# A hybrid decoder layer on one core: the gate row of the residual applied after the output projection, gate rows by row sums through memory, merges on VectorE, and two blocks of the output projection computed channel by channel

## The chip, the cores and the metric

The kernel runs on one core of a Trainium2 chip. The metric is the device time of one execution in microseconds (us), the median over runs. A profile is one further execution, recorded instruction by instruction; its own time, and the span of its instructions, are given beside the runs below.

The engines, as the profile names them: PE is TensorE (matmuls, transposes), PEld its weight loads, DVE is VectorE, ACT is ScalarE, POOL is GpSimd, and SP is the engine from which most transfers (DMA) are issued.

## The reference, cut to what matters

One decoder layer for 512 tokens of width 1024, all in float32. A conditioning vector `c` gives six rows of 1024 numbers, `mod = c @ w_ada + b_ada`: shift, scale and gate of each of the two sub-layers. Two causal attention branches of eight heads each (a forgetting softmax, FoX, and a stick-breaking one, sb) read one input projection.

```python
mod = c @ w_ada + b_ada
sh1, sc1, gt1, sh2, sc2, gt2 = split(mod, 6)
u = x * (1.0 + sc1) + sh1
q_a, k_a, v_a, f_a, q_b, k_b, v_b, g_a, g_b = split(u @ w_in)
y_fox = forgetting_attention(q_a, k_a, v_a, log_sigmoid(f_a + b_forget))
y_sb = stick_breaking_attention(q_b, k_b, v_b)
merged = sigmoid(g_a) * (y_fox @ w_fox_proj) + sigmoid(g_b) * (y_sb @ w_sb_proj)
attn_out = merged @ w_o
x = layer_norm(ALPHA * x + (1.0 + gt1) * attn_out, ln1_g, ln1_b)
u2 = x * (1.0 + sc2) + sh2
h_gate, h_val = split(causal_depthwise_conv(u2 @ w_up, conv_w, conv_b))
ffn_out = (silu(h_gate) * h_val) @ w_down
x = layer_norm(ALPHA * x + (1.0 + gt2) * ffn_out, ln2_g, ln2_b)
```

The gate row `1 + gt1` multiplies the columns of `attn_out`, so it may as well multiply the columns of `w_o`; the same holds for `1 + gt2` and `w_down`.

## The kernel before, in words

**Precision.** Every operand of a large matmul is split into a rounded high part (ScalarE, `hi_of`, L75) and the remainder (VectorE, `lo_of`, L78), and each product is three matmuls, high by high, high by low and low by high (`mm3`, L110 to L112). A tile of weights (128x1024 raw numbers, from SP through four buffers `raw`) thus costs one pass of ScalarE and one of VectorE before TensorE can use it (`wh`, `wl`, three buffers).

**Stages in time.** (1) Up to 50 us: shift and scale rows of the first sub-layer by row sums on VectorE (`mod_col`, L164: multiply a 128x1024 tile of transposed `w_ada` with the broadcast `c`, sum along the row, L169, add the bias, L172), and the first input projections. (2) Up to 302 us: sixteen heads, stick-breaking first. Each head has three steps: `stage_a` (scores and softmax or stick-breaking weights), `stage_b` (transposes of the weights and their split), `stage_c` (product with v). Between the steps `fill` issues a set number of matmuls from `stream`, a list of generators: the remaining projections (`proj`), the gate projections (`add_gate`, 24 matmuls each, then a sigmoid), and the branch projections (`bproj`, 12 matmuls each). `lim` says how far the list may be used at each head. (3) The rest of the list, then the output projection with its layer norm by blocks of 128 tokens (`o_main`), each block transposed back (`o_turn`), to 410 us. (4) The up-projection, 44 tiles of 24 matmuls, to 652 us. (5) The down-projection and the second layer norm.

**The gate rows.** `ada_proc` handles the 32 remaining tiles of `w_ada`, one item of the weight stream each. Items 8 to 23 are row sums for shift and scale of the second sub-layer. Items 0 to 7 (first gate) and 24 to 31 (second gate) are accumulated on VectorE into a 128x512 tile, two half-tiles per item (L525, L530); `ada_split` splits the sum into two parts, and `ada_sum` adds it up over the 128 partitions with two matmuls against a matrix of ones (L548, L549), adding the bias row (L551). That leaves the gate row in every partition (`gt`).

**Output projection.** GpSimd multiplies each of the eight weight tiles of `w_o` by `gt` (`wo_proc`, L576) before the split. GpSimd also adds the two gated branches (`merge`, L676), whose result is split into `mh` and `ml`, eight channel tiles. `o_main(i)` then runs 48 matmuls for block i, channel after channel (L819 to L821), with VectorE's residual and statistics behind them (L824, L825, L828). The weight tiles of `w_down` are multiplied by the second gate row on GpSimd in the same way (L588).

**What sets the order.** A scheduler lays out each engine's instructions once, at build time; only SP's transfers keep the order of the program. Engines run their own list in order, and wait for each other by semaphores. VectorE and ScalarE serve the heads and the weight stream from one list each, so a weight tile or a row sum that stands ahead of a head's tile in that list is done first.

Of the kernel before, what the change touches and what calls it, by code (L numbers as in the profile page):

```python
# [45 lines left out]
def layer_kernel(ctx: ExitStack, tc: tile.TileContext, out, xT, x, cT, crow, wa0, wa1, bcol, bgt, w1, wct, wv, bf,  # L46
# [36 lines left out]
    cTs = const([P, KT], F32, "cTs")  # L83
    bcols = const([P, 4, KT], F32, "bcols")
# [7 lines left out]
    onesr = const([P, P], F32R, "onesr")  # L92
    V.tensor_copy(onesr, ones)
# [9 lines left out]
    modc = const([P, 4, KT], F32, "modc")  # L103
    modr = const([P, 4, KT, 2], F32, "modr")
# [70 lines left out]
    def first_load(j):  # L175
# [17 lines left out]
        if j == 1:  # L193
            nc.sync.dma_start(cTs, cT)
            nc.sync.dma_start(bfs, bf)
        pend[j] = [wa, xt, r]

    def first_acc(j):
        wa = pend[j][0]
        if j == 0:  # L200
            for q in (1, 3):
                V.tensor_scalar_add(bcols[:, q, :], bcols[:, q, :], 1.0)
        mod_col(0, j, wa[0], 2 if j == 0 else 1)
        return mod_col(1, j, wa[1], 2 if j == 0 else 1)
# [20 lines left out]
    def first_mod(j):  # L225
        wa, xt = pend[j][0:2]
        sh, sc = modc[:, 0, j : j + 1], modc[:, 1, j : j + 1]
# [281 lines left out]
    def gt_tile(i):  # L509
        t = cons.tile([P, D], F32, name=f"gt{i}", tag="gt")  # L510
        nc.sync.dma_start(t, bgt[i : i + 1, :].broadcast_to([P, D]))
        return t

    gt = [None, None]
    ada_st = {}

    def ada_proc(n):
        def f(r):
            if 8 <= n < 24:
                mod_col(2 + (n - 8) // 8, n % 8, r)  # L520
                return
            g, q = n // 4, n % 4
            if q == 0:
                ada_st[g] = z(F32, "ac2")
                V.tensor_scalar_mul(ada_st[g], r[:, 0:512], cTs[:, 0:1])  # L525
            acc = ada_st[g]
            for e in range(2):
                k = 2 * q + e
                if k > 0:
                    V.scalar_tensor_tensor(acc, r[:, e * 512 : (e + 1) * 512], cTs[:, k : k + 1], acc, ALU.mult, ALU.add)  # L530
        return f

    def ada_split(g, n):
        weights(n, 0)
        acc = ada_st[g]
        ah, al = z(F32R, "ach"), z(F32R, "acl")
        hi_of(ah, acc)
        lo_of(al, acc, ah)
        ada_st[g] = ah, al
        yield 0  # L540

    def ada_sum(g):
        ah, al = ada_st.pop(g)
        ps = bank()
        i = 0 if g < 2 else 1
# [496 lines left out]
```

## Time and profile before

| | |
|---|---|
| median of 3 runs | 779.21 us (778.69 to 779.27) |
| the profiled execution's own time | 776.24 us |
| its span of instructions | 774.2 us |
| PE busy | 755.8 us (98%) |
| DVE busy | 554.2 us (72%) |
| ACT busy | 351.1 us (45%) |
| POOL busy | 144.5 us (19%) |

The page has the busy time of each engine, groups of instructions by line with the mean time of one, the waits (who waited for whom), the chain that ended last, and each engine's timeline. A matmul of 512 columns is recorded with some 0.39 us, since matmuls overlap; what it takes of TensorE is the distance to the next one. TensorE's granted clock stands in the tables by stretch of time, where 1.00 is full speed.

### The profile page before, as it was taken

Reading aid. Unit: us, or ns where it says so; the run is one execution under the profiler, and the core shown is the slowest. Engines: PE = TensorE matmul, PEld = TensorE weight load, DVE = VectorE, ACT = ScalarE, POOL = GpSimd, SP = SyncE. Lnnn points to the kernel's source line nnn. Section 1 sums busy time; section 2 is a strip of 40 time slices with the busy share of each in tenths; the row PEclk is TensorE's granted clock in tenths of the full one; section 3 lists DMA queues with packets and bytes.
Section 4 is the critical chain, followed back from the end, with each engine's and each line's share of the span. In section 5 each row is a group of like instructions: output and inputs, shape, how many; then the busy total and the mean of one; then the engine's idle time right before and its main releaser. Section 6 shows DMA issues by size and latency. Waiting matters only on the chain.

```text
span 774.2 us, 9555 instructions
## 1 busy us (share of the span) xinstructions
PE 755.8 (98%) x3567; PEld 625.0 (81%) x3567; DVE 554.2 (72%) x854; ACT 351.1 (45%) x584; POOL 144.5 (19%) x106
## 2 busy tenths in 40 slices
PE   8998999999999999998999999999999999999995
PEld 5886887888888888886889888888888888888885
DVE  6979999966687876666656887777666665534666
ACT  3357596727666564444125334444444433222300
POOL 1030002001010012363000680000000043945500
PEclk9999999999999999999999999999999999999999
DMA  8961254353333324544301615353332314332302
GB/s 316 403 207 33 78 187 134 119 193 105 113 107 109 136 82 136 166 166 155 118 1 55 218 56 162 109 190 136 110 108 82 109 54 164 113 105 83 108 28 81
DMA packets 30960, 99.41 MB, mean 128 GB/s; under 512 B 4257, under 2 KB 4769, under 8 KB 30914
## 3 DMA queue, kind: packets, MB, share of 16 engines
q1 hardware_dynamic: 30402, 98.74, 37.4%
q8 instruction: 28, 0.46, 0.2%
q0 software_dynamic: 512, 0.07, 0.1%
q14 instruction: 18, 0.15, 0.1%
HBM read 96.62 MB, written 2.10 MB: 128 GB/s over the span
## 4 chain that ended last, share of the span: by engine, by line
PE 77%; DVE 8%; ACT 6%; DMA 3%; issue 3%; POOL 2%; DVEq 0%; POOLq 0%; ACTq 0%; SPq 0%
PE ps L110 14%; PE ps L111 14%; PE ps L112 14%; PE ps L253 5%; PE ps L935 5%; PE ps L934 5%; PE ps L933 5%; PE ps L496 2%; DVE wl L78 2%; ACT wh L75 2%; PE ps L820 2%; PE ps L821 1%; PE ps L478 1%; PE ps L819 1%; DMA raw<-in_wo 1%
## 5 line engine op out<-in xcount | busy, mean ns | idle before, releaser
L78 DVE TENSOR_TENSOR wl<-raw,wh 128x1024 fp32r<-128x1024 f32 (+2 forms) x106 | 145.8, 1375 | 99.8 <-ACT wh L75 99.4
L75 ACT ACTIVATE wh<-raw 128x1024 fp32r<-128x1024 f32 (+2 forms) x106 | 110.3, 1041 | 109.3 <-PE ps L935 38.4
L110 PE MATMUL ps<-u2h,wh 128*128 128x512 f32 (+1 forms) x376 | 141.4, 376 | 0.0
L111 PE MATMUL ps<-u2l,wh 128*128 128x512 f32 (+1 forms) x376 | 141.2, 376 | 0.0
L112 PE MATMUL ps<-u2h,wl 128*128 128x512 f32 (+1 forms) x376 | 141.2, 375 | 0.0
L588 POOL TENSOR_TENSOR raw<-raw,gt 128x1024 f32<-128x1024 f32 x22 | 60.3, 2755 | 190.1 <-DVE gt L551 157.6
L110 PE MATMUL ps<-uh,wh 128*128 128x512 f32 x232 | 92.6, 399 | 0.0
L112 PE MATMUL ps<-uh,wl 128*128 128x512 f32 x232 | 90.9, 392 | 0.0
L111 PE MATMUL ps<-ul,wh 128*128 128x512 f32 x232 | 90.7, 391 | 0.0
L111 PEld LDWEIGHTS ps<-u2l,wh 128*128 128x128 f32 x376 | 70.8, 188 | 12.9
L110 PEld LDWEIGHTS ps<-u2h,wh 128*128 128x128 f32 x376 | 70.8, 188 | 12.8
L112 PEld LDWEIGHTS ps<-u2h,wl 128*128 128x128 f32 x376 | 70.8, 188 | 12.8
L112 PEld LDWEIGHTS ps<-uh,wl 128*128 128x128 f32 x232 | 43.6, 188 | 9.3
L110 PEld LDWEIGHTS ps<-uh,wh 128*128 128x128 f32 x232 | 43.6, 188 | 8.3 <-ACT pt L454 0.3
L111 PEld LDWEIGHTS ps<-ul,wh 128*128 128x128 f32 x232 | 43.7, 188 | 8.0
L934 PE MATMUL ps<-wl,hh 128*128 128x512 f32 x128 | 49.8, 389 | 0.0
L933 PE MATMUL ps<-wh,hh 128*128 128x512 f32 x128 | 49.8, 389 | 0.0
L935 PE MATMUL ps<-wh,hl 128*128 128x512 f32 x128 | 49.8, 389 | 0.0
L75 ACT ACTIVATE hh<-cv 128x512 fp32r<-128x512 f32 x22 | 13.9, 632 | 59.6 <-DVE cv L913 59.6
L912 ACT ACTIVATE cv<-cv 128x512 f32<-128x512 f32 x22 | 13.9, 632 | 54.8 <-DVE cv L907 54.8
L576 POOL TENSOR_TENSOR raw<-raw,gt 128x1024 f32<-128x1024 f32 x8 | 20.1, 2517 | 80.9 <-DVE m L78 42.2
L906 DVE SCALAR_TENSOR_TENSOR cv<-ps,cw,cv 128x511 f32<-128x511 f32 x44 | 32.7, 743 | 2.3 <-ACT cv L905 2.3
(190 smaller groups left out, 1449.8 us busy)
## 6 DMA issues: line engine op xcount, KB each, us to landing
raw<-in_wup SPq DMA_DIRECT2D x44, 512.0 KB, 3.3
raw<-in_wa SPq DMA_DIRECT2D x32, 512.0 KB, 3.3
raw<-in_wct SPq DMA_DIRECT2D x29, 512.0 KB, 3.8
raw<-in_wdn SPq DMA_DIRECT2D x22, 512.0 KB, 3.2
wa<-in_wa SPq DMA_DIRECT2D x14, 512.0 KB, 7.3
raw<-in_wp SPq DMA_DIRECT2D x8, 512.0 KB, 3.2
raw<-in_wo SPq DMA_DIRECT2D x8, 512.0 KB, 4.2
raw<-in_w SPq DMA_DIRECT2D x7, 452.0 KB, 8.0
```

The lines of the kernel that those rows point to most:

```text
L75: S.activation(o, i, AF.Copy, scale=scale)
L78: return V.tensor_tensor(o, i, fl(hi), ALU.subtract)
L110: PE.matmul(ps, wh, ah, start=first, stop=False)
L111: PE.matmul(ps, wh, al, start=False, stop=False)
L112: PE.matmul(ps, wl, ah, start=False, stop=last)
L253: PE.matmul(grp[g], w, u, start=j == 0 and n == 0, stop=j == KT - 1 and n == (1 if g == 7 else 2))
L576: G.tensor_tensor(r, r, gt[0], ALU.mult)
L588: G.tensor_tensor(r, r, gt[1], ALU.mult)
L906: V.scalar_tensor_tensor(t[:, 1:], ps[:, 0:511], cw[:, n, 1:2], t[:, 1:], ALU.mult, ALU.add)
L933: PE.matmul(ps, hh[j][:, tb], w[0], start=first, stop=False)
L934: PE.matmul(ps, hh[j][:, tb], w[1], start=False, stop=False)
L935: PE.matmul(ps, hl[j][:, tb], w[0], start=False, stop=last)
```

## The change

The first gate row is no longer multiplied into the weights: `wo_proc` only splits, and `o_main` multiplies the finished product in PSUM by the gate row on VectorE, 128x512 at a time. Both gate rows are now computed like the other rows, by `mod_col`: one row sum of 128x1024 per item. That leaves the row as a column of 128 partitions by 8; `gt_tile` writes it to memory with a transfer on GpSimd's queue and reads it back broadcast to all partitions with a second one. The accumulation, split and ones-matmuls are gone. The second gate row is still multiplied into `w_down` by GpSimd. The sum of the branches moves from GpSimd to VectorE. The five gate projections that stood between the branch projections now stand ahead of them. The output projection of blocks 0 and 1 is done channel by channel in four PSUM banks (`o_part`), 12 matmuls per channel, two places behind the branch projection that makes the channel; blocks 2 and 3 stay in `o_main`. `o_main(2)` moves ahead of `o_turn(0)`.

```diff
-    onesr = const([P, P], F32R, "onesr")
-    V.tensor_copy(onesr, ones)
...
         if j == 0:
-            for q in (1, 3):
-                V.tensor_scalar_add(bcols[:, q, :], bcols[:, q, :], 1.0)
+            V.tensor_scalar_add(bcols[:, 2:6, :], bcols[:, 2:6, :], 1.0)
...
-    def gt_tile(i):
-        t = cons.tile([P, D], F32, name=f"gt{i}", tag="gt")
-        nc.sync.dma_start(t, bgt[i : i + 1, :].broadcast_to([P, D]))
+    MODS = (4, 1, 3, 5)
+    rows = ctx.enter_context(tc.tile_pool(name="rows", bufs=1, space=bass.MemoryType.DRAM))
+
+    def gt_tile(w):
+        row = rows.tile([1, D], F32, name=f"row{w}", tag=f"row{w}")
+        t = cons.tile([P, D], F32, name=f"gt{w}", tag="gt")
+        with nc.allow_non_contiguous_dma("one row of 1024 numbers"):
+            G.dma_start(row.rearrange("o (k p) -> p (o k)", p=P), modc[:, w, :])
+        G.dma_start(t, row.broadcast_to([P, D]))
         return t
...
     def ada_proc(n):
         def f(r):
-            if 8 <= n < 24:
-                mod_col(2 + (n - 8) // 8, n % 8, r)
-                return
-            g, q = n // 4, n % 4
-            if q == 0:
-                ada_st[g] = z(F32, "ac2")
-                V.tensor_scalar_mul(ada_st[g], r[:, 0:512], cTs[:, 0:1])
-            acc = ada_st[g]
-            for e in range(2):
-                k = 2 * q + e
-                if k > 0:
-                    V.scalar_tensor_tensor(acc, r[:, e * 512 : (e + 1) * 512], cTs[:, k : k + 1], acc, ALU.mult, ALU.add)
+            w, col = MODS[n // KT], n % KT
+            mod_col(w, col, r)
+            if col == KT - 1 and w > 3:
+                gt[w - 4] = gt_tile(w)
         return f
-    def ada_split(g, n):
...
-    def ada_sum(g):
...
     def wo_proc(r):
-        G.tensor_tensor(r, r, gt[0], ALU.mult)
...
     def merge(j):
         def f(m):
-            G.tensor_tensor(m, m, ma[j], ALU.add)
+            V.tensor_tensor(m, m, ma[j], ALU.add)
...
+    wos, acc2 = [], []
+
+    def o_step(ps, i, e, k):
+        tb = slice(i * P, (i + 1) * P)
+        PE.matmul(ps, mh[k][:, tb], woh[k][e], start=k == 0, stop=False)
+        PE.matmul(ps, mh[k][:, tb], wol[k][e], start=False, stop=False)
+        PE.matmul(ps, ml[k][:, tb], woh[k][e], start=False, stop=k == KT - 1)
+
+    def o_part(k):
+        if k == 0:
+            acc2.extend([bank(), bank()] for _ in range(2))
+        weights(wos[k], 1)
+        for i in range(2):
+            for e in range(2):
+                o_step(acc2[i][e], i, e, k)
+            yield 6
...
     for j in range(3):
         add_gate(0, j)
     marks["y0"] = len(stream)
-    flush_sum(1 << 30)
+    for j in range(3, KT):
+        add_gate(0, j)
+    skip[0] = 0
+    add_ada(24 - adas[0])
     for j in range(KT):
         add_bproj(0, j, merge(j))
-        if j < 5:
-            add_wo()
-        if j + 3 < KT:
-            add_gate(0, j + 3)
...
+        if j:
+            wos.append(add_item(wo[j - 1], wo_proc))
+            if j > 1:
+                stream.append((o_part, (j - 2,)))
+    wos.append(add_item(wo[KT - 1], wo_proc))
+    for k in (KT - 2, KT - 1):
+        stream.append((o_part, (k,)))
...
-        cut = 6 if i == 0 else KT
-        for e, ks in ((0, range(cut)), (1, range(cut)), (0, range(cut, KT)), (1, range(cut, KT))):
...
+        ps2 = acc2[i] if i < 2 else [bank(), bank()]
         for e in range(2):
             ps = ps2[e]
+            if i > 1:
+                for k in range(KT):
+                    o_step(ps, i, e, k)
+            V.tensor_tensor(ps, ps, gt[0][:, e * 512 : (e + 1) * 512], ALU.mult)
             V.scalar_tensor_tensor(xn[e], xn[e], ALPHA, ps, ALU.mult, ALU.add)
...
-    weights(last_wo, 0)
     o_main(0)
     o_main(1)
+    o_main(2)
     o_turn(0)
-    o_main(2)
     o_turn(1)
...
-            if n in (20, 36):
-                g = 6 if n == 20 else 7
-                list(ada_split(g, wai[4 * g + 3]))
-            if n in (22, 38):
-                list(ada_sum(6 if n == 22 else 7))
```

On the host, the tiles of `w_ada` for the gates are packed transposed like the others, and the bias rows come as one array of six columns.

**How instructions move, first place: VectorE between the first and the third head.** `s_` and `m_` are the split parts of q and k that the next scores wait for, `om_` the stick-breaking factors, `wl_` the low part of a weight tile. Before, q of the second pair of heads, and then its k:

```order
L305 SCALAR_TENSOR_TENSOR fq_542<-ps_110,bfs,fq_541 8x512
L347 SCALAR_TENSOR_TENSOR s_79_559<-ps_105,s_79_559 64x512
L347 SCALAR_TENSOR_TENSOR s_80_562<-ps_105,s_80_562 64x512
L457 SCALAR_TENSOR_TENSOR om_610<-om_610,zer 128x127
L457 SCALAR_TENSOR_TENSOR om_610<-om_610,zer 128x383
```

```order
L78 TENSOR_TENSOR m_2_526<-ps_565,m_114_692 64x512
L78 TENSOR_TENSOR wl_704<-raw_572,wh_703 128x1024
L78 TENSOR_TENSOR m_3_527<-ps_565,m_115_696 64x512
L78 TENSOR_TENSOR vv_713<-ps_106,vv_713 128x2x128
L78 TENSOR_TENSOR vv_716<-ps_107,vv_716 128x2x128
```

The same two pieces of the change:

```order
L342 SCALAR_TENSOR_TENSOR s_79_556<-ps_102,s_79_556 64x512
L166 SCALAR_TENSOR_TENSOR raw_824,modr<-raw_824,cbc 128x1024
L342 SCALAR_TENSOR_TENSOR s_80_559<-ps_102,s_80_559 64x512
L452 SCALAR_TENSOR_TENSOR om_607<-om_607,zer 128x127
L452 SCALAR_TENSOR_TENSOR om_607<-om_607,zer 128x383
```

```order
L78 TENSOR_TENSOR m_2_521<-ps_562,m_114_689 64x512
L78 TENSOR_TENSOR wl_701<-raw_569,wh_700 128x1024
L169 TENSOR_TENSOR modc<-modr,bcols 128x1
L78 TENSOR_TENSOR wl_827<-raw_698,wh_826 128x1024
L78 TENSOR_TENSOR m_3_522<-ps_562,m_115_693 64x512
L78 TENSOR_TENSOR vv_710<-ps_103,vv_710 128x2x128
```

The first row sum of a gate (L166 in the change) now stands between the two parts of q, and its bias together with a second weight tile now stands ahead of the second part of k.

**Second place: TensorE at the end of the branch projections.** `yh`/`yl` are the attention result, `ps_3435` and `ps_3473` the last branch projection's bank. Before:

```order
L112 MATMUL ps_3435<-yh_3022,wl_3348 128x512
L819 MATMUL ps_3489<-woh_3032,mh_3058 128x512
L820 MATMUL ps_3489<-wol_3034,mh_3058 128x512
L821 MATMUL ps_3489<-woh_3032,ml_3059 128x512
L819 MATMUL ps_3489<-woh_3070,mh_3119 128x512
```

Now:

```order
L109 MATMUL ps_3473<-yh_3003,wl_3424 128x512
L650 MATMUL ps_3281<-woh_3427,mh_3400 128x512
L651 MATMUL ps_3281<-wol_3429,mh_3400 128x512
L652 MATMUL ps_3281<-woh_3427,ml_3401 128x512
L650 MATMUL ps_3282<-woh_3428,mh_3400 128x512
```

Before, the whole product of block 0 began behind the last branch projection; now three pieces of 12 matmuls are left there, for channels 5, 6 and 7, and blocks 2 and 3 follow.

**Third place: VectorE on block 3**, the last to be normalised (`xn`) and transposed back. Before, the end of that block and the start of the up-projection:

```order
L792 SCALAR_TENSOR_TENSOR mv_3797<-mv_3797 128x1
L78 TENSOR_TENSOR u2l<-uf_740_3808,u2h 128x4x128
L828 TENSOR_SCALAR xn_3738<-xn_3738,mv_3797 128x512
L828 TENSOR_SCALAR xn_3739<-xn_3739,mv_3797 128x512
L78 TENSOR_TENSOR u2l<-uf_741_3809,u2h 128x4x128
L842 TENSOR_SCALAR uf_756_3900<-ps_3898,gm,bm 128x128 x4
```

Now, first the rows around the second half of the block's residual, then the end of the block:

```order
L796 BN_STATS st_3713<-xn_3711 128x6
L78 TENSOR_TENSOR wl_3814<-raw_3805,wh_3813 128x1024
L78 TENSOR_TENSOR wl_3821<-raw_3807,wh_3820 128x1024
L794 TENSOR_TENSOR ps_3717<-ps_3717,gt_1736 128x512
L813 TENSOR_SCALAR uf_730_3784<-ps_3782,gm,bm 128x128
L795 SCALAR_TENSOR_TENSOR xn_3712<-xn_3712,ps_3717 128x512
```

```order
L765 SCALAR_TENSOR_TENSOR mv_3772<-mv_3772 128x1
L78 TENSOR_TENSOR wl_3851<-raw_3809,wh_3850 128x1024
L799 TENSOR_SCALAR xn_3711<-xn_3711,mv_3772 128x512
L799 TENSOR_SCALAR xn_3712<-xn_3712,mv_3772 128x512
L166 SCALAR_TENSOR_TENSOR raw_3848,modr<-raw_3848,cbc 128x1024
L813 TENSOR_SCALAR uf_748_3881<-ps_3879,gm,bm 128x128 x4
```

The splits of the first three tiles of `w_up` (`wl_3814`, `wl_3821`, `wl_3851`), which VectorE had done ahead of block 0, now stand around block 3; the multiplication by the gate row (L794 in the change) stands ahead of each residual, and a row sum ahead of the copies of block 3's transposes (`uf_748`).

71 lines of the change are left out of this document (12 added, 59 removed).

## The prediction, made before the changed kernel had run

> **What bounds the kernel now.** I read the page's busy times and chain first.
>
> ```profile
> span 774.2 us, 9555 instructions
> PE 755.8 (98%) x3567; PEld 625.0 (81%) x3567; DVE 554.2 (72%) x854; ACT 351.1 (45%) x584; POOL 144.5 (19%) x106
> PE 77%; DVE 8%; ACT 6%; DMA 3%; issue 3%; POOL 2%; DVEq 0%; POOLq 0%; ACTq 0%; SPq 0%
> ```
>
> PE is busy for 98% of the span and holds 77% of the chain. VectorE is second with 72%, POOL has 19%: work taken from POOL is worth nothing by itself, and work given to VectorE costs something only where PE then waits. So I went on to PE's waits (total, number, longest).
>
> ```profile
> PE ps L478 <- DVE m L78: 3.3, 1, 3.3
> ...
> PE ps L819 <- ACT woh L75: 1.5, 1, 1.5
> PE ps L819 <- ACT mh L75: 1.2, 1, 1.2
> PE ps L821 <- DVE ml L78: 0.6, 1, 0.6
> PE ps L422 <- DVE m L78: 0.4, 1, 0.4
> ...
> PE ps L820 <- DVE wol L78: 0.3, 1, 0.3
> ```
>
> Two places stand out: 3.3 us before the transposes of the second head pair (L478), and four waits of 3.6 us together at the start of the output projection (L819 to L821), for a merged channel and for a weight tile. Then the stretches of 2 us around both (length; busy us of PE, PEld, DVE, ACT, POOL; granted clock; DMA), and one long stretch.
>
> ```profile
> 72.00:74.00 2.00, 2.00 (x10) 1.91 (x9) 1.91 (x5) 2.00 (x4) 0.00 (x0) 0.50 0.55 203
> 354.00:356.00 2.00, 1.02 (x5) 0.52 (x3) 0.33 (x1) 1.42 (x2) 0.72 (x1) 1.00 0.86 231
> 356.00:358.00 2.00, 1.17 (x4) 0.70 (x5) 2.00 (x3) 1.20 (x3) 0.00 (x0) 1.00 0.95 297
> 358.00:360.00 2.00, 2.00 (x8) 1.54 (x7) 1.30 (x3) 0.00 (x0) 1.22 (x1) 0.62 1.01 367
> 360.00:362.00 2.00, 2.00 (x7) 1.59 (x6) 0.87 (x2) 1.53 (x2) 0.44 (x1) 0.53 0.41 156
> 76.00:126.00 50.00, 50.00 (x261) 42.02 (x259) 46.36 (x73) 38.61 (x69) 3.98 (x8) 1.00 0.36 117
> ```
>
> After each place the clock is granted at half for a while. At 358 to 362 us the missing clock is 2 x 0.38 + 2 x 0.47 = 1.70 us of full speed, so 3.4 us at half; behind the early wait it stands at 0.50. A second price of a wait is thus 1.7 us of PE, and here a stretch with PE busy for only 1.02 and 1.17 of 2 us, with no long wait in it, was followed by it. [...]
>
> **The change part by part.** The sum is made against the profiled execution: 776.24 us, of which 774.2 is span, so 2.0 lies around it; the median of the runs, 779.21, is 3.0 above that execution.
>
> *1. The matmuls against ones go.*
>
> ```profile
> L548 PE MATMUL ps<-ach,onesr 128*128 128x512 f32 x4 | 1.6, 392 | 0.0
> L549 PE MATMUL ps<-acl,onesr 128*128 128x512 f32 x4 | 1.6, 392 | 0.0
> 354.41 0.39 PE L820 MATMUL ps<-wol,mh 128*128 128x512 f32 x1
> 354.64 0.39 PE L821 MATMUL ps<-woh,ml 128*128 128x512 f32 x1
> 357.56 0.50 PE L821 MATMUL ps<-woh,ml 128*128 128x512 f32 x1 [0.61 <-DVE ml L78]
> 364.04 0.39 PE L821 MATMUL ps<-woh,ml 128*128 128x512 f32 x1
> 366.74 0.50 PE L820 MATMUL ps<-wol,mh 128*128 128x512 f32 x1 [0.30 <-DVE wol L78]
> ```
>
> Two matmuls of this size stand 0.23 us apart. Eight go: -1.8 us. The output projection's 192 matmuls are only moved.
>
> *2. End of the branch projections.* Before, from 354.64 to 357.56 three matmuls passed in 2.92 us instead of 0.68, from 364.04 to 366.74 two in 2.70 instead of 0.45: 4.5 us lost, and 1.5 to 1.7 more at half clock; I take -6.0 for both. Whether the change wins that depends on its new covers. A channel's product now comes two places behind its branch projection, so between the end of that projection and the first matmul of its `o_part` lie one more projection and one more `o_part`, 24 matmuls or 5.4 us. VectorE and ScalarE must meanwhile multiply by the gate, add, round and subtract, four passes over 128x512 of about 0.69 (L824's duration, quoted under 5), and one low part of a weight tile:
>
> ```profile
> L78 DVE TENSOR_TENSOR wl<-raw,wh 128x1024 fp32r<-128x1024 f32 (+2 forms) x106 | 145.8, 1375 | 99.8 <-ACT wh L75 99.4
> L576 POOL TENSOR_TENSOR raw<-raw,gt 128x1024 f32<-128x1024 f32 x8 | 20.1, 2517 | 80.9 <-DVE m L78 42.2
> ```
>
> 4 x 0.69 + 1.38 = 4.1 of 5.4 us. POOL's 2.52 us ahead of each `wo` split, the sum of the two, goes as well, which shortens exactly the chain that L819 waited for. If one step still missed, it would be by well under a microsecond; bounds -6.2 and -4.0.
>
> *3. The early wait.*
>
> ```profile
> 71.55 0.70 PE L478 MATMUL ps<-ident,pt 128*128 128x128 f32 x3 [3.27 <-DVE m L78]
> 57.67 0.69 DVE L347 SCALAR_TENSOR_TENSOR s<-ps,s 64x512 fp32r<-64x512 f32 x1 [0.66 <-ACT s L75]
> 68.77 0.67 DVE L78 TENSOR_TENSOR m<-ps,m 64x512 fp32r<-64x512 f32 x1
> 69.36 1.21 DVE L78 TENSOR_TENSOR wl<-raw,wh 128x1024 fp32r<-128x1024 f32 x1
> 70.70 0.69 DVE L78 TENSOR_TENSOR m<-ps,m 64x512 fp32r<-64x512 f32 x1
> L169 DVE SCALAR_TENSOR_TENSOR raw<-raw,cbc 128x1024 f32<-128x1024 f32 x16 | 19.6, 1222 | 7.9 <-DMA raw<-in_wa 7.8
> ```
>
> From 57.67 on VectorE runs without a gap to the second `m` (70.70), for which PE waited. The order puts a row sum (1.22, and 0.08 to read it out) between the parts of q: 0.66 of it fills an idle, the rest, 0.6, delays. A bias of 0.1 and a second weight tile (1.2) come ahead of the second `m`: 1.3. If the first figure partly vanishes at the scans, `m` is 1.6 us late and the wait grows from 3.3 to 4.9. Queued behind it are the scores and their whole head. Against it: the half-speed stretch, set off at the same time as before, would run partly during the longer idle and cost some 0.7 less. I take +1.0; the bounds are +0.3 (the tile is not ready, and the order's row costs little) and +3.3 (1.6 plus another 1.7 of half clock).
>
> *4. The third head.* One more row sum stands ahead of its `m`, 1.3 us at worst, where PE waited 0.4 before; the gate row's own wait at the bank (L551) goes. +0.2 (0 to +1.3).
>
> *5. Block 3.* Three blocks of the layer norm now reach VectorE almost at once.
>
> ```profile
> 402.89 0.40 PE L821 MATMUL ps<-woh,ml 128*128 128x512 f32 x1
> 403.13 1.03 PE L838 MATMUL ps<-ident,xn 128*128 128x128 f32 x8
> 409.76 1.03 PE L838 MATMUL ps<-ident,xn 128*128 128x128 f32 x8
> 407.04 1.00 DVE L828 TENSOR_SCALAR xn<-xn,mv 128x512 f32<-128x512 f32 x2
> L824 DVE SCALAR_TENSOR_TENSOR xn<-xn,ps 128x512 f32<-128x512 f32 x8 | 5.5, 689 | 16.0 <-PE ps L821 16.0
> L825 DVE BATCH_NORM_STATS2 st<-xn 128x6 f32<-128x512 f32 x8 | 5.6, 694 | 0.3
> L842 DVE TENSOR_SCALAR uf<-ps,gm,bm 128x128 f32<-128x128 f32 x16 | 6.0, 391 | 2.2 <-PE ps L838 2.2
> ```
>
> Of block 3, the last matmul ended at 403.29, normalising at 408.04 (4.8 us), and PE came to its transposes at 409.76 without waiting: it had 6.6 us of cover from 403.13. Now the chain has a gate multiplication more (0.69, like L824's row), a weight tile ahead of normalising (1.2, row of 69.36), and VectorE's backlog. A block costs 6 x 0.69 + 1.0 + some 0.3 of small rows = 5.5; a turn 4 x 0.39 + 2 x 0.69, some 2.8, part of which fits into pauses, so 2.5. From the point where block 0's banks are full, 6 matmuls ahead of the end of `o_part(7)`, to the end of block 3's products PE takes 102 x 0.227 + 2 turns of about 1.0 = 25.2 us. VectorE has in that time three blocks (16.5), half of the fourth (2.1), two turns (5.0) and two weight tiles (2.4): 26.0. It ends 0.8 to 1.0 late. So 4.8 + 0.7 + 1.2 + 1.0 = 7.7 against 6.6: a wait of 1.1. I take +1.0; bounds 0 (small rows hide, ScalarE takes more) and +2.8 (1.1 plus 1.7 of half clock, as after the stretches of 354 to 358). Late behind it are only the turn's copies and the first tiles of the second half.
>
> *6. Start of the second half.* A row sum stands ahead of block 3's copies (1.3), which PE's transposes and the remaining columns wait for: PE has the next tiles' matmuls of the other blocks to do. +0.3 (0 to +0.8).
>
> *7. The gate row through memory.* No such write stands in the trace. The nearest rows are of GpSimd's 4 KB rows:
>
> ```profile
> 143.78 0.52 POOL L328 DMA_DIRECT2D m<-chi  x1 [0.29 <-POOL m L326]
> s<-chi POOLq DMA_DIRECT2D x8, 4.0 KB, 2.0
> q0 software_dynamic: 512, 0.07, 0.1%
> ```
>
> 512 packets over 16 transfers are 32 packets each: 0.52 us to issue, 2 us to land. 1024 elements of 4 bytes in as many packets would be 32 times that at most: 17 us on GpSimd, 64 to landing, and the broadcast read behind it; at the least it is like the row itself. The first row's sums are done at about 145 us and the first use is past 370, the second's are done at about 557 and used by the down-projection from about 620 (GpSimd) and 652 on (PE). Decay rows queue behind it on GpSimd, with 50 us to spare. 0; it turns into a cost from some 65 us on. GpSimd's merges and `wo` products, 1.6 and 2.5 us a piece, had lain off the path but for step 2.
>
> Sum: -1.8 - 6.0 + 1.0 + 0.2 + 1.0 + 0.3 = -5.3. Span 768.9, profiled execution 770.9, **median 773.9**, said as 774.
>
> **The rivals.**
>
> *A: no new wait.* ScalarE and the pauses absorb the backlog, and the early `m` is late only by what the half clock gives back: -1.8 - 6.0, span 766.4, **771.4**. For it: PE 50.00 of 50 us busy from 76 to 126 with VectorE at 46.36, so the added rows found no one to delay there. Against: from 57.67 to 70.70 VectorE had no gap.
>
> *B: each new wait brings its half clock.* Steps 3 and 5 at their upper ends: +3.3 + 2.8 instead of +2.0, and 0.2 + 0.3 as before, **778.0**. For it: the row of 354 to 358, where PE was half busy. Against: the 1.5 us wait at 364 to 366 was followed by none.
>
> *C: slower; row sums ahead of the heads.* Six row sums of 1.3 us stand early on VectorE, at the heads of 57 to 131 us, ahead of the tiles that the next scores wait for. If PE waits for each in full, that is 7.8 us and one more half clock 1.7: with -7.8 and block 3's and the second half's 1.3, +3.0, **782.2**. It decides from the point where PE's new waits before 131 us exceed 6.5 us. For it: VectorE at 46.36 of 50 us, 93%. Against: PE waited nowhere in those 50 us, and ran off a lead.
>
> *D: the gate row is late*, or GpSimd is held by it beyond 85 us, so that block 0 or the down-projection stops: each us beyond costs one, and from 6 us on the sum is above no change, **780** and more. For it: elements of 4 bytes. Against: over 60 us of spare at both.
>
> **How the numbers follow.** Forecast 0.55, A 0.15, B 0.15, C 0.10, D 0.05. The forecast's own range is 772 to 776. The range is 771 to 778: A and B stand at its edges, C and D are left out. A measurement of this kernel can tell some 0.2%, 1.6 us, from no change, that is, 777.6 to 780.8. Faster hold the forecast and A with little loss and some of B: 0.74; no change the rest of B and pieces of D: 0.13; slower C and D: 0.13.
>
> **What would show it right or wrong.** Step 1: PE's instructions fall by eight matmuls. Step 2: no wait on `mh`, `ml`, `woh` or `wol`, and granted clock 1.00 at the end of the branch projections. Step 3: the wait at the transposes of the second pair is 4 to 5 us, released by `m` or by a weight tile. Step 5: a wait of about 1 us at block 3's transposes, released by VectorE; VectorE without a gap before it. Step 7: the write's time to landing under 65 us, and no wait on `gt`. The prediction is wrong if PE's waits before 131 us come to more than 8 us in all, if the half rate shows at a third place, or if PE waits for the gate row.

## The result, and the profile after

The changed kernel takes **770.39 us** (median of 4 runs, 769.29 to 770.88), the kernel before on the same chip 778.95 (777.8 to 779.27): a ratio of 0.9891, 95% interval 0.9874 to 0.9908. That is 8.6 us less. Forecast were 774.0 and a gain of 5.2; the time lies 0.6 us under the low end of the range.

The page after: span and instructions, busy times, and the chain that ended last by engine.

```profile
span 768.5 us, 9512 instructions
PE 752.1 (98%) x3559; PEld 624.6 (81%) x3559; DVE 546.5 (71%) x876; ACT 350.4 (46%) x580; POOL 113.0 (15%) x94
PE 91%; DVE 4%; ACT 4%; issue 1%; DMA 0%; DVEq 0%
```

The span fell from 774.2 to 768.5, by 5.7 us. The sum in the prediction gave 768.9 for it. So the sum of the steps came out to 0.4 us, in part by luck, since single terms were off by up to 2.1 us both ways (below), and the miss in the time lies between the profiled executions and the medians: before, the profiled execution (776.24) was 2.7 us faster than the median on the day of the result; after, 770.30 stands against 770.39. PE's share of the chain rose from 77 to 91%.

PE's waits after (total, number, longest):

```profile
PE ps L473 <- DVE m L78: 4.9, 1, 4.9
PE ps L156 <- DMA cbr<-in_crow: 2.5, 1, 2.5
PE ps L416 <- ACT m L75: 0.4, 2, 0.2
PE ps L809 <- DVE xn L799: 0.2, 1, 0.2
```

The four waits of the output projection are gone, all 3.6 us. The early wait grew from 3.3 to 4.9 us, as told. Block 3's transposes waited 0.2 us. In stretches of 2 us (length; busy PE, PEld, DVE, ACT, POOL; granted clock; DMA):

```profile
72.00:74.00 2.00, 0.39 (x2) 0.42 (x3) 1.94 (x4) 1.36 (x5) 0.00 (x0) 0.64 0.62 209
74.00:76.00 2.00, 2.00 (x10) 1.91 (x9) 2.00 (x6) 0.87 (x2) 0.00 (x0) 0.50 0.74 258
76.00:78.00 2.00, 2.00 (x11) 1.48 (x10) 0.58 (x2) 0.76 (x2) 0.00 (x0) 0.50 0.14 57
78.00:80.00 2.00, 2.00 (x11) 1.92 (x10) 2.00 (x5) 2.00 (x6) 0.00 (x0) 0.65 0.00 0
354.00:356.00 2.00, 2.00 (x11) 1.65 (x10) 0.53 (x1) 0.00 (x0) 0.00 (x0) 1.00 0.00 0
358.00:360.00 2.00, 2.00 (x10) 1.68 (x9) 2.00 (x4) 1.64 (x4) 0.00 (x0) 1.00 0.00 0
```

At the end of the branch projections PE is full and its clock whole. Behind the early wait the missing clock is 2 x (0.36 + 0.50 + 0.50 + 0.35) = 3.4 us, so 6.8 us at half rate, two stretches in a row, where before there was one.

Where the 5.7 us came from, by the times at which PE reached the same matmul (from the two traces' rows, before and after):

| stretch | before | after | difference |
|---|---|---|---|
| start to the first transposes after the early wait | 71.55 | 73.61 | +2.1 |
| to the end of the half rate behind it | 76.07 | 79.13 | +1.0 |
| to the last head's last matmul | 302.12 | 303.44 | -1.7 |
| to the output projection's last matmul | 402.89 | 397.61 | -6.6 |
| to the up-projection's last matmul | 645.98 | 640.14 | -0.6 |
| to the last matmul | 766.07 | 760.16 | -0.1 |

That is -5.9 us; 0.2 of it is lost again behind the last matmul. Of the -1.7, 0.9 are the first gate's four ones-matmuls and some 0.4 the third head's wait, which is gone.

### The profile page after: what moved, and what is told of

Read it like the earlier page. It is cut to its first block, busy times and chain, and to the rows that moved or that the text cites. A ratio compares the mean times of both kernels' runs of the same rounds, so it can differ in the third digit from the quotient of the medians.

```text
span 768.5 us, 9512 instructions
## 1 busy us (share of the span) xinstructions
PE 752.1 (98%) x3559; PEld 624.6 (81%) x3559; DVE 546.5 (71%) x876; ACT 350.4 (46%) x580; POOL 113.0 (15%) x94
## 4 chain that ended last, share of the span: by engine, by line
PE 91%; DVE 4%; ACT 4%; issue 1%; DMA 0%; DVEq 0%
PE ps L107 17%; PE ps L108 17%; PE ps L109 17%; PE ps L248 6%; PE ps L898 5%; PE ps L899 5%; PE ps L897 5%; PE ps L491 2%; PE ps L473 2%; PE ps L652 2%; PE ps L650 2%; PE ps L651 2%; PE ps L416 2%; PE ps L417 1%; PE ps L391 1%; ACT wh L75 1%
## 5 line engine op out<-in xcount | busy, mean ns | idle before, releaser
L78 DVE TENSOR_TENSOR wl<-raw,wh 128x1024 fp32r<-128x1024 f32 (+2 forms) x106 | 142.2, 1343 | 120.5 <-ACT wh L75 120.1
L109 PEld LDWEIGHTS ps<-u2h,wl 128*128 128x128 f32 x376 | 70.8, 188 | 12.7
L107 PEld LDWEIGHTS ps<-u2h,wh 128*128 128x128 f32 x376 | 70.8, 188 | 12.7
L558 POOL TENSOR_TENSOR raw<-raw,gt 128x1024 f32<-128x1024 f32 x22 | 60.1, 2747 | 81.0 <-DVE hl L78 50.9
L166 DVE SCALAR_TENSOR_TENSOR raw<-raw,cbc 128x1024 f32<-128x1024 f32 x32 | 39.0, 1219 | 12.0 <-DMA raw<-in_wa 11.9
```

Of the source, the lines that this page charges most:

```text
L78: return V.tensor_tensor(o, i, fl(hi), ALU.subtract)
L107: PE.matmul(ps, wh, ah, start=first, stop=False)
L109: PE.matmul(ps, wl, ah, start=False, stop=last)
L166: V.scalar_tensor_tensor(wt[:, c], wt[:, c], 1.0, cbc[:, c], ALU.mult, ALU.mult, accum_out=raw[:, e : e + 1])
L558: G.tensor_tensor(r, r, gt[1], ALU.mult)
```

## The experiments

Each run was compared with the kernel before on the same chip. "Clock" is the mean over all executions of a kernel of its granted clock.

| kernel | median us | lowest to highest | ratio to before (95%) | clock |
|---|---|---|---|---|
| before, all executions of the three comparisons | 778.42 | 775.72 to 781.26 (61) | | 0.9921 |
| `again`: before, unchanged | 778.35 | 776.80 to 779.66 (12) | 0.9999 (0.9990 to 1.0008) | 0.9928 |
| `after2`: the change, unchanged | 770.03 | 769.32 to 770.91 (4) | 0.9889 (0.9872 to 0.9906) | 0.9932 |
| `o_late2`: order of blocks and gates undone | 769.48 | 769.17 to 770.57 (4) | 0.9887 (0.9872 to 0.9901) | 0.9930 |
| `pool`: both tasks back on GpSimd | 777.20 | 775.97 to 777.96 (12) | 0.9978 (0.9968 to 0.9988) | 0.9920 |
| `late_row`: `o_late2`, merges on GpSimd | 769.37 | 768.80 to 770.75 (5) | 0.9886 (0.9869 to 0.9904) | 0.9928 |
| `late_merge`: `o_late2`, gate times weights on GpSimd | 771.96 | 770.06 to 772.21 (5) | 0.9907 (0.9891 to 0.9923) | 0.9936 |
| `late_both`: `o_late2`, both on GpSimd | 777.51 | 776.04 to 779.27 (12) | 0.9994 (0.9981 to 1.0007) | 0.9895 |
| `late_ones`: before, both tasks on VectorE | 770.54 | 769.69 to 771.64 (6) | 0.9897 (0.9880 to 0.9914) | 0.9940 |
| `skip6`: the change, row sums later | 771.82 | 770.05 to 772.17 (5) | 0.9909 (0.9894 to 0.9923) | 0.9928 |
| `skip6_row`: `skip6`, gate row transposed first | 768.12 | 767.34 to 768.89 (4) | 0.9864 (0.9847 to 0.9881) | 0.9940 |
| `best1`: `o_late2` with both of these | 768.37 | 767.40 to 768.57 (5) | 0.9868 (0.9851 to 0.9885) | 0.9942 |
| `best2`: `best1`, merges on GpSimd | 771.20 | 770.56 to 772.06 (6) | 0.9908 (0.9892 to 0.9924) | 0.9942 |

### What the usual execution of the kernel before has more

The kernel before, unchanged.

> The kernel before, unchanged, to learn what its usual executions have that the profiled one (776.24 us, two stretches of half clock of 3.4 us) had not. Theory G (grid): stretches of half rate lie on a fixed grid of 3.413 us, which begins anywhere against the program; the waits at 68 us and at 354 to 367 us set off two stretches in a lucky position and three or four in others, at 1.7 us each. Then executions near 779 us have a mean granted clock of 0.991 to 0.992 against 0.994 in the profiled one, and spans of 777. Rival E (edges): the 2.7 us are lost at the first loads or outside the span; then the clock is 0.994 in all executions, whatever their time.

Its spans with their clock: executions at a mean clock of 0.994 have a median of 777.7 us (20 of the 61), those at 0.990 and less 778.95 (16). So G holds, in part: slower executions have the lower clock. Over the 61, the clock takes 6.1 us of full speed (the mean of one less the clock, times the span), against 4.8 in the profiled execution and 4.9 in the changed kernel's. At most these 1.3 us of the 2.2 that separate 776.24 from 778.42 are thus accounted for. At most, because this figure also counts the half rate behind the last matmul, where TensorE has no matmul left: 1.4 of the 4.8 us here, and 1.4 to 2.7 us in the fourteen profiled executions. The rest stays open: even the executions at 0.994 are 1.4 us above that profiled one, which was among the lowest of all.

What makes the number of stretches vary is seen where the stretches begin. In the traces' clock records a stretch lasts 3.413 us, and the two in a row in the change 6.827. They begin on a grid of that length: in the profiled execution before, the second stretch begins 286.72 us after the first, 84 times 3.4133, and the half rate behind the last matmul 699.73 us after it, 205 times; in the change the latter begins 692.91 us after the first stretch, 203 times; in `skip6` two stretches begin 109.22 us apart, 32 times. Where the grid lies against the program differs from execution to execution (half rate from 70.92 to 73.17 us in the table). Behind the early wait, from the clock records and PE's first matmul after the wait, in six of the fourteen profiled executions of this study:

| profiled execution | wait, us | PE resumes | half rate begins | stretches |
|---|---|---|---|---|
| before | 3.3 | 71.55 | 71.74 | 1 |
| `skip6` | 3.3 | 71.95 | 73.17 | 1 |
| `best2` | 3.3 | 71.92 | 72.99 | 1 |
| `late_ones` | 3.3 | 71.61 | 71.46 | 2 |
| `skip6_row` | 3.3 | 71.34 | 70.92 | 2 |
| the change | 4.9 | 73.61 | 72.57 | 2 |

In all fourteen, a second stretch followed where PE was still waiting when the half rate set in, and none where it was running again. So a wait of 3.3 us costs one stretch or two, by where the grid falls, and in all seven executions with 4.9 us it cost two. This is what fourteen executions have in common; no run moved the grid on purpose.

### Which part won: the order, or GpSimd's two tasks

First the channel-wise product was undone, and the gate projections put back between the branch projections:

```diff
-    for j in range(3, KT):
-        add_gate(0, j)
     ...
-            if j > 1:
-                stream.append((o_part, (j - 2,)))
+        if j + 3 < KT:
+            add_gate(0, j + 3)
     ...
-        ps2 = acc2[i] if i < 2 else [bank(), bank()]
+        ps2 = [bank(), bank()]
```

> Of the change, only the channel-wise product of blocks 0 and 1 and the place of the five gate projections are undone (both as before: all four blocks after the last branch projection, gates between the projections); gate row on the result, row sums and merges on VectorE stay. Theory O (the cover of 24 matmuls per channel is what won): the waits for a merged channel come back, 3 to 6 us, 774 to 777 us. Rival P (what won is that GpSimd's 2.5 us no longer stand ahead of each weight split, and its 1.6 us not ahead of each merged channel): within 1.5 us of the change, 769 to 772 us, no wait over 0.5 us at the output projection.

769.48 us: theory O, the step as the prediction told it, falls. The only wait over 0.3 us left besides the first load is the early one:

```profile
PE ps L473 <- DVE m L78: 4.9, 1, 4.9
PE ps L156 <- DMA cbr<-in_crow: 2.3, 1, 2.3
PE ps L416 <- ACT m L75: 0.3, 2, 0.2
```

Then the opposite: the new order stays, GpSimd's two tasks come back.

```diff
-            V.tensor_tensor(m, m, ma[j], ALU.add)
+            G.tensor_tensor(m, m, ma[j], ALU.add)
     def wo_proc(r):
+        G.tensor_tensor(r, r, gt[0], ALU.mult)
     ...
-            V.tensor_tensor(ps, ps, gt[0][:, e * 512 : (e + 1) * 512], ALU.mult)
```

> The change with two parts undone: GpSimd adds the branches again and multiplies the first gate row into the weights of the output projection again; the channel-wise product, the row sums and the place of the gates stay. Theory O: the cover of 5.4 us holds GpSimd's merge too, no wait at the output projection over 0.5 us, and block 3 has one pass less: 769.5 to 771.5 us. Rival P: waits for a merged channel or a weight tile of 2 us or more in all come back: 772.5 us or more.

777.20 us. The waits, in this kernel's line numbers (L651 to L653 are the three matmuls of the output projection):

```profile
PE ps L653 <- DVE ml L78: 2.9, 2, 1.5
...
PE ps L652 <- DVE wol L78: 1.2, 2, 0.8
PE ps L651 <- ACT mh L75: 0.7, 1, 0.7
PE ps L651 <- ACT woh L75: 0.6, 1, 0.6
```

5.4 us: a cover of 24 matmuls per channel does not hold GpSimd's work. So the tasks were the cost, on this order as on the old one. Which of the two? On the order of `o_late2`, merges alone on GpSimd:

> The kernel of the run o_late2 (all four blocks after the last branch projection, gates between them, 769.5 us) with the merges back on GpSimd: so of GpSimd's two tasks only the multiplication of the weights by the gate row is taken away. Theory W (the 2.5 us of GpSimd ahead of each weight split are the cost, the merge of 1.3 to 1.6 us is covered): no wait for a weight tile, at most 1.2 us for a merged channel, 769.5 to 771.5 us. Theory M (the merge is the cost): waits for mh and ml of 2 us and more and a stretch of half clock, 773 us or more.

769.37 us and no such wait. And the weights alone on GpSimd:

> The kernel of the run o_late2 with the multiplication of the output projection's weights by the gate row back on GpSimd, merges on VectorE, no multiplication of the result. Theory W: waits for woh and wol of 1.5 to 5 us, 772 to 776 us. Theory M: no such waits, 769 to 770.5 us.

771.96 us, between the ranges of the two theories, but not by waits of 1.5 us and more at the output projection: its trace loses 1.5 us against `late_row` within the first 79 us (0.9 of it before 12 us) and only 0.3 after, at the last weight tile. What moved the start there stays open. So on this order either task alone is hidden, the weights just so. Both together:

> The kernel of the run o_late2 with both tasks back on GpSimd (merges, and the first gate row times the output projection's weights): of the change only the gate rows by row sums through memory are left. With one of the two tasks back, no wait was seen at the output projection (769.4 and 772.0 us). Theory J (the tasks cost only together: GpSimd's 2.4 and 1.3 us stand in each other's way and stretch VectorE's passes): waits at L650 to L652's matmuls of 2 to 5 us come back and the executions spread over 4 us again, 774 to 779 us. Rival R (what took the waits away is that the gate row's accumulation no longer competes with the branch projections' VectorE work): no such wait, 768.5 to 772 us.

777.51 us, and the interval of its ratio holds 1: the row sums, all that is left of the change here, are worth nothing that can be told. Its waits (L651 to L653 again the output projection):

```profile
PE ps L651 <- ACT woh L75: 3.1, 1, 3.1
...
PE ps L651 <- ACT mh L75: 0.8, 1, 0.8
PE ps L653 <- DVE ml L78: 0.6, 1, 0.6
...
PE ps L652 <- DVE wol L78: 0.3, 1, 0.3
```

And the two tasks taken away with nothing else changed in the kernel before:

```diff
     def wo_proc(r):
-        G.tensor_tensor(r, r, gt[0], ALU.mult)
     ...
-            G.tensor_tensor(m, m, ma[j], ALU.add)
+            V.tensor_tensor(m, m, ma[j], ALU.add)
     ...
+            V.tensor_tensor(ps, ps, gt[0][:, e * 512 : (e + 1) * 512], ALU.mult)
```

> The kernel before with two edits only: the gate row multiplies the result on VectorE, and VectorE adds the branches. Gate rows by accumulation and ones-matmuls, order and early head pairs are as before. Theory J: the four waits at the output projection go, 6 us, and with them the spread: profiled execution and median within 1 us of each other, 769 to 772 us, early wait 3.3 us. Rival R: the waits stay, 776 to 779 us. Between the two kernels' medians the row sums' own worth is then seen: 769.5 (o_late2) less this.

770.54 us, ratio 0.9897: two edits give what the whole change gives, and with them the spread shrinks from 5.5 to 2 us and the mean clock rises to 0.9940. That the spread comes from the waits at the output projection would fit, but is not shown: six executions stand here against 61, and `pool`, with 5.4 us of such waits, spreads over only 2.0 us in 12. (The profiled execution was here the slowest of six, 771.64, so the expected 1 us between it and the median was missed by 0.1.)

**Why only together.** ScalarE's rows show it. In all four kernels its list ends in this stage with the same pieces: a tile of the up-projection (`wh<-raw`), the merged channels 5, 6 and 7 (`mh`) with another `wh` between, and behind the last `mh` the last weight tile of the output projection (`woh`). With neither task on GpSimd (`o_late2`):

```profile
346.70 1.06 ACT L75 ACTIVATE wh<-raw 128x1024 fp32r<-128x1024 f32 x1 [1.44 <-DMA raw<-in_wup]
348.10 0.64 ACT L75 ACTIVATE mh<-sg 128x512 fp32r<-128x512 f32 x1 [0.33 <-DVE sg L638]
...
354.04 0.64 ACT L75 ACTIVATE mh<-sg 128x512 fp32r<-128x512 f32 x1 [0.83 <-DVE sg L638]
354.58 1.14 ACT L75 ACTIVATE woh<-raw 128x512 fp32r<-128x512 f32 x2
```

With both (`late_both`):

```profile
354.56 1.06 ACT L75 ACTIVATE wh<-raw 128x1024 fp32r<-128x1024 f32 x1 [3.79 <-DMA raw<-in_wup]
355.53 0.61 ACT L75 ACTIVATE mh<-sg 128x512 fp32r<-128x512 f32 x1
...
364.70 0.63 ACT L75 ACTIVATE mh<-sg 128x512 fp32r<-128x512 f32 x1 [2.66 <-POOL sg L639]
365.24 1.14 ACT L75 ACTIVATE woh<-raw 128x512 fp32r<-128x512 f32 x2
365.91 0.49 PE L651 MATMUL ps<-woh,mh 128*128 128x512 f32 x1 [3.09 <-ACT woh L75]
```

The first row is the key. ScalarE waits for a tile of `w_up`, which nobody needs for another 50 us, because its load came late; the channels that PE needs now stand behind it. Then each `mh` waits for its merge. The last `woh` starts at 354.58 with neither task, at 358.28 with the merges on GpSimd (the `wh` row at 347.00), at 360.81 with the weights there (353.12, so the load is what the weights delay), at 365.24 with both: 3.7, 6.2 and 10.7 us late. Of the 6.2, 1.5 are the late start of that whole trace, so the two alone add up to 8.4, and both together cost more than the sum. The first half of that tile is rounded some 0.6 us after its start. PE reads it at 360.72 with neither task (5.5 us of reserve), at 360.76 and 362.19 with one (1.9 and 0.8 us left), and with both only at 365.91, after 3.1 us of waiting. One task alone stays inside the reserve, both overrun it. This is read from the rows: no run took the `wh` out of ScalarE's way.

The loads of the up-projection's first three tiles were issued from 344.7 us on, in `o_late2` from 339.3. SyncE, which issues them, waits for a free buffer: one with a tile of `w_o` is free when its low part `wol` is made, and that stands behind GpSimd's multiplication. SyncE's waits for `wol` (total, number, longest), first in `o_late2`, then with the weights on GpSimd (`late_merge`; `late_both` has 20.4 us, `late_row` 12.7; totals of the whole run, which do not say how much each load was late by it):

```profile
SPq L123 <- DVE wol L78: 11.3, 4, 4.0
```

```profile
SPq L123 <- DVE wol L78: 21.8, 5, 8.6
```

GpSimd's multiplications also slow VectorE beside them, a pass of 0.69 us to 2.77. Rows by group, `ml` (two operands in SBUF) and the gate multiplication (one in PSUM), in `late_both` from 302 to 372 us, and then `ml` in `o_late2`:

```profile
L78 DVE TENSOR_TENSOR ml<-sg,mh 128x512 fp32r<-128x512 f32 x8 | 11.8, 1478 | 13.6 <-ACT mh L75 13.6
...
L541 DVE TENSOR_TENSOR sg<-ps,sg 128x512 f32<-128x512 f32 x8 | 5.5, 684 | 0.0
```

```profile
L78 DVE TENSOR_TENSOR ml<-sg,mh 128x512 fp32r<-128x512 f32 x8 | 5.5, 689 | 2.2 <-ACT mh L75 2.2
```

The mean of 1478 ns hides two sizes. Of the four rows from 344 us on, three took 0.68 to 0.69 us, as without GpSimd. The fourth took 2.77; it began while a multiplication of weights ran on GpSimd and ended 0.55 us after it:

```profile
346.96 2.40 POOL L547 TENSOR_TENSOR raw<-raw,gt 128x1024 f32<-128x1024 f32 x1 [0.52 <-DMA raw<-in_wo]
347.14 2.77 DVE L78 TENSOR_TENSOR ml<-sg,mh 128x512 fp32r<-128x512 f32 x1 [2.07 <-ACT mh L75]
```

The pass that reads PSUM stayed at 684 ns on average. The kernel before has both kinds of pass beside such multiplications (L576). `ml`, begun at 347.80, took 2.23 us and ended 0.55 us after the multiplication; the pass with an operand in PSUM, begun at 343.52 within the second of two, took 0.68:

```profile
340.62 5.24 POOL L576 TENSOR_TENSOR raw<-raw,gt 128x1024 f32<-128x1024 f32 x2 [3.31 <-DMA raw<-in_wo]
...
347.07 2.41 POOL L576 TENSOR_TENSOR raw<-raw,gt 128x1024 f32<-128x1024 f32 x1
...
343.52 0.68 DVE L570 TENSOR_TENSOR sg<-ps,sg 128x512 f32<-128x512 f32 x1
347.80 2.23 DVE L78 TENSOR_TENSOR ml<-sg,mh 128x512 fp32r<-128x512 f32 x1 [3.60 <-ACT mh L75]
```

With the merges alone on GpSimd `ml` took 688 ns (`late_row`). It comes behind its own merge there, so this does not show what a pass that falls on a merge would take.

### The early wait, and what came of shortening it

The first row sum two places later in the stream, so that it and the second weight tile no longer stand ahead of the second part of k:

```diff
-    skip = [4]
+    skip = [6]
```

> The change, with the first row sum two places later in the stream of weights, so that neither it nor a second weight tile stands ahead of the second part of k of the second pair on VectorE. Theory S (step 3 as told): the early wait falls from 4.9 to about 3.3 us and one of the two stretches of half clock behind it goes in most executions: 1.6 to 3.3 us less than the change, 767 to 769 us. Rival L: the sums, moved later, delay later heads as much: 770 us, with new waits after 82 us.

771.82 us, above the ranges of both theories and no faster than the change (the intervals overlap). In the profiled execution both parts of theory S came true, a wait of 3.3 us and a single stretch, and PE was some 2.5 us ahead of the change from 80 us on. But all of it was lost at once at 181 us, and 1.5 us more behind it:

```profile
PE ps L416 <- ACT m L75: 3.4, 2, 3.2
PE ps L473 <- DVE m L78: 3.3, 1, 3.3
```

with a stretch of half clock behind. That looks like rival L, but the rows before it point elsewhere. VectorE's row sum at 169.66 waited 8.77 us for a tile, and the transfers nearly stood still (last two columns: DMA share and GB/s):

```profile
169.66 1.23 DVE L166 SCALAR_TENSOR_TENSOR raw<-raw,cbc 128x1024 f32<-128x1024 f32 x1 [8.77 <-DMA raw<-in_wa]
...
156.00:158.00 2.00, 2.00 (x11) 1.65 (x10) 1.76 (x3) 0.00 (x0) 0.95 (x1) 1.00 0.57 178
...
160.00:162.00 2.00, 2.00 (x10) 1.66 (x9) 0.44 (x2) 0.66 (x2) 0.00 (x0) 1.00 0.48 27
162.00:164.00 2.00, 2.00 (x10) 1.67 (x9) 0.00 (x0) 0.00 (x0) 0.00 (x0) 1.00 1.10 37
164.00:166.00 2.00, 2.00 (x10) 1.65 (x10) 0.00 (x0) 0.00 (x0) 0.00 (x0) 1.00 0.30 20
...
row<-modc POOLq DMA_DIRECT2D x2, 4.0 KB, 10.8
```

20 to 37 GB/s instead of 178 from 160 to 168 us, the time in which the gate row went to memory number by number (issued at 156.2; 10.8 us to landing is the median of its two writes), while a 512 KB tile asked for at 157.5 was under way. The change's own write, 8 us earlier, shows the same: 25 to 35 GB/s from 152 to 160 us, and 303 and 410 in the two stretches after it. VectorE waited 5.6 us for a tile there, but PE's matmuls went on. To tell this from rival L, the row was transposed first by one small matmul and then written in 8 rows of 512 bytes; the matmul stands at about 302 us.

```diff
+        ps = bank()
+        PE.transpose(ps[0:KT, 0:P], modc[:, w, :], ident)
+        r = const([KT, P], F32, f"rowt{w}")
+        S.activation(r, ps[0:KT, 0:P], AF.Copy)
     ...
-            G.dma_start(row.rearrange("o (k p) -> p (o k)", p=P), modc[:, w, :])
+        G.dma_start(row.rearrange("o (k p) -> (o k) p", p=P), r)
     ...
+    stream.append((row_tr, (4,)))
```

> The kernel of the run skip6 (first row sum two places later, 771.8 us) in which the gate row is first transposed by one small matmul (8x128 from 128x8), so that the transfer to memory writes 8 rows of 512 bytes instead of 1024 single numbers. In skip6 the packets of the other transfers fell from some 70 to 100 per us to 4 to 11 for the 9 us that the row's write took (158.5 to 168), a weight tile landed 9 us late, and PE waited 3.2 us at 181 us with a stretch of half clock behind. Theory Q (the write of single numbers holds up all transfers): the loads run on while the row is written, the wait at 181 us and its stretch go, 766.5 to 768.5 us. Rival V (VectorE's row sums ahead of the first FoX keys are the cause): the wait of about 3 us at 181 us stays, 770.5 to 772 us.

768.12 us, 1.9 less than the change on the same chip (770.03), and their executions do not overlap. Theory Q's time and rows came out, and rival V falls: the same row sums stand ahead of the same keys. The wait at 181 us is gone, and the write lands in 3.9 us instead of 10.8:

```profile
row<-rowt POOLq DMA_DIRECT2D x2, 4.0 KB, 3.9
...
PE ps L473 <- DVE m L78: 3.3, 1, 3.3
```

(The write was also moved, from 156 to 303 us. The run does not separate the two, so that the shape of the write and not its place is what helped is not shown; at its new place the traffic went on at 135 GB/s and more.) This profiled execution had two stretches of half clock behind the same 3.3 us wait where `skip6` had one, as in the table of the grid.

The yardstick of that comparison:

> The changed kernel again, unchanged, as the yardstick on this chip, and for the spread of its executions: by theory G one place with waits is left, so the executions lie within 2 us of each other at a mean clock of 0.992 to 0.994, where those of the kernel before lay 4 us apart at 0.988 to 0.994. 769.5 to 770.9 us.

Its four executions lie within 1.6 us, at a mean clock of 0.992 to 0.994, as G has it.

### Putting the parts together

> The kernel of the run o_late2, with the first row sum two places later and the gate row transposed before it is written. Both worked on the other order (768.1 us). If the parts add: the 769.5 of o_late2 less 1.9: 767 to 768.5 us, early wait 3.3 us, no wait at 180 us.

768.37 us, as expected, and no better than `skip6_row` (768.12): the block order makes no difference here either. These two beat the kernel before by some 10 us, and the change by 2; of these 2, only `skip6_row` was measured beside the change on one chip.

> The kernel of the run best1 with the merges on GpSimd. Theory J says that one task on GpSimd is covered: as best1 within 0.7 us. If VectorE's merge passes were the cheaper way even alone: 0.7 us or more slower than best1.

771.20 us, 2.8 more than `best1`, where at most 0.7 was expected: the expectation failed. The merges alone on GpSimd, covered in `late_row`, are not covered here:

```profile
PE ps L653 <- DVE wol L78: 1.1, 2, 0.9
PE ps L652 <- ACT woh L75: 0.9, 1, 0.9
```

(L652 and L653 are the first two matmuls of the output projection.) Its row sums stand later, and ScalarE's list has the last two weight tiles together behind the last `mh`, at 358.87. So a shift of the list uses up the reserve that hides one task, 1.9 us in `late_row`.

## Why the prediction was right or wrong, step by step

1. **Ones-matmuls, -1.8.** Right: 8 matmuls fewer on PE's count (3567 to 3559). But `late_ones`, which keeps them, is at 0.9897 against 0.9887 for `o_late2`, within the intervals: with the longer early wait that the row sums brought, the gate rows' new way is worth nothing that can be told.
2. **End of the branch projections, -6.0.** The size was right in the profiled executions (-6.6), the reason was not. The step put the gain on the new covers, 24 matmuls per channel, and named GpSimd's 2.5 us only as a help. `o_late2` keeps the gain without the covers, `pool` loses most of it with them. What counted was that both GpSimd tasks left a chain that, on the order of `o_late2`, had room for one.
3. **The early wait, +1.0.** The wait came out at 4.9 us to the tenth, released by `m` as told. The term was mis-sized by the clock: the half rate was expected to overlap the longer idle and cost 0.7 less; it came twice. That is +3.1 in all by PE's times, near the upper bound of +3.3; 0.3 of it was lost in the first 13 us already.
4. **The third head, +0.2.** No wait remains there: some 0.4 us were won instead.
5. **Block 3, +1.0.** Measured 0.2. The order of events was right, the backlog was not there: VectorE was idle before block 2's second half and began the end of block 3 0.2 us after its products.

```profile
385.39 0.70 DVE L794 TENSOR_TENSOR ps<-ps,gt 128x512 f32<-128x512 f32 x1 [0.92 <-PE ps L652]
...
398.16 0.69 DVE L794 TENSOR_TENSOR ps<-ps,gt 128x512 f32<-128x512 f32 x1
...
404.24 1.00 DVE L799 TENSOR_SCALAR xn<-xn,mv 128x512 f32<-128x512 f32 x2
404.84 1.11 PE L809 MATMUL ps<-ident,xn 128*128 128x128 f32 x8 [0.21 <-DVE xn L799]
```

6. **Second half, +0.3.** No wait, so 0.
7. **The gate row, 0.** Right for the time, wrong in what it costs: it was priced by its own landing alone. That the other transfers would crawl beside it (25 to 35 GB/s for 8 us in the change) was not thought of; in the change it falls where PE had a reserve.

The sum of -5.3 against -5.7 is thus partly luck: the early wait cost 2.1 us more than its term, and the other stretches together 2.5 us less than theirs.

**The step that put the time outside the range** is the last line of the sum, "Span 768.9, profiled execution 770.9, median 773.9": it took the 3.0 us between profiled execution and median before as a constant of both kernels. After the change it was 0.1. With that in place of 3.0 the sum gives 771.0, the low end of the range. The 3.0 were mostly the draw of one execution: of the 61 others of the kernel before only three were faster than 776.24, and their median lies 2.2 above it. Why that kernel's executions lie where they do is known only in part. Up to 1.3 us of the 2.2 lie in the clock. That the rest are the waits at the output projection and the half rate behind them, which the change removed, is a guess: `late_both`, which has these waits, spreads over 3.2 us at a clock of 0.9895, and the kernels without them over 2.2 us or less at 0.993 to 0.994, with 4 to 6 executions each against 12. Against it stands `pool`, with such waits and a spread of 2.0 us in 12 executions; its profiled execution shows no half rate there. So the cause stays open. Rival A, at 771.4, was the nearest case by its time, but not by its reason: the early wait did grow.

## What to carry to other kernels

A profiled execution is one draw. Where it is faster than the median by more than the runs scatter, that difference is not a constant to be added to the changed kernel too; more executions of the kernel before show first how far they spread. An engine at 19% can set the end of a stage: follow the in-order list of the engine behind it, where a tile for a later stage, held up by a late load, blocks the piece that is needed now. Before a wait is paid for with a new order, try whether taking one link out of the chain does it: here two edits were worth the whole change.

## What the runs showed of the hardware that was not expected

- While 1024 numbers of 4 bytes were written to memory, the other transfers of the core crawled: 20 to 37 GB/s for some 8 us in `skip6`, 25 to 35 in the change; a 512 KB tile landed after 12 us instead of 3.3. In rows of 512 bytes, at another place, the same 4 KB landed in 3.9 us instead of 10.8, and the traffic went on at 135 GB/s and more. Whether the size of the pieces or the place made the difference is not shown.
- The half rate came in stretches of 3.413 us on a grid that lay elsewhere in each execution (behind the early wait the half rate began at 70.92 to 73.17 us): the same 3.3 us of wait cost one stretch or two.
- A pass of VectorE over two SBUF operands that began beside a multiplication on GpSimd ended only after it (2.77 us in `late_both` and 2.23 in the kernel before, instead of 0.69); a pass with an operand in PSUM, begun beside one in the kernel before, was not slowed (0.68 us).
